# A gated delta net's second pair of head groups gets tiles of its own, and the block solutions move to GpSimd

## The chip, the cores and the metric

The kernel is a decoder of two blocks on one core of a Trainium2 chip. The metric is the device time of one execution in microseconds; the profile shows one execution, its span from the first to the last instruction. TensorE (PE) does the matmuls, VectorE (DVE), ScalarE (ACT) and GpSimd (POOL) work on tiles, SyncE (SP) issues most DMAs; GpSimd issues some. Each engine works through a list of its own in order, and waits on semaphores for the others.

## The reference, cut to what matters

The first block takes 256 tokens of width 1024 and has two mixers side by side. The change is within the first of them, a gated delta rule over 8 heads in chunks of 64:

```
proj = rmsnorm(x) @ w_in          # q, k, v, z, two gates, and the second mixer's inputs
k, q = l2norm(silu(conv(.)));  v = silu(conv(.))
decay = exp(G_i - G_j) below the diagonal;  a_mat = beta * (k k^T) * decay, strictly lower
sol   = (I + a_mat)^-1 @ [v * beta, k * beta * exp(G)]        # triangular_solve, per head and chunk
for each chunk:  v_new = value - k_cum @ s
                 o = (q * exp(G)) @ s + (q k^T * decay) @ v_new
                 s = s * chunk_decay + (k * exp(g_last - G))^T @ v_new
y_a = (rmsnorm(o) * silu(z)) @ w_proj_gdn
y_b = (forgetting attention) @ w_proj_fox
h = x + (sigmoid(gate_a) * y_a + sigmoid(gate_b) * y_b) @ w_out
x = h + relu(h_normed @ w_up)^2 @ w_down
```

A second block (two swiglu layers and another attention mixer) follows and is not touched.

## The kernel before, in words

Activations lie transposed, features on partitions and the 256 tokens on the free axis. Each weight matrix comes in by DMA on SP's queue as `raw`; ACT rounds it to a high part `wh` (L220), DVE subtracts to get the low part `wl` (L221, 128x1024 at a time), and PE does three matmuls of 128x128 by 128x256 for each pair of tiles: high by high, high by low, low by high (L258 to L260 and L349 to L351). A matmul of this kind is called a projection matmul below; one weight unit of 1024 columns is 24 of them.

The first block's code is a set of lines (Python generators) which a planner interleaves: the main line yields the PE time that it puts out, and side lines (the head groups, the solutions) advance between, after the delays that they yield. So the order on each engine is fixed when the program is built. `PLAN` lists what the main line projects: q, k and v of a head group ("heads"), two heads' z, or a sixteenth of the two gates. After it come the second mixer's output projection, then that of the delta rule in two parts: the first (L1135, L1138) takes groups 0 and 1, the second (L1147, L1148) groups 2 and 3.

The eight heads are four groups of two, and two groups are a pair. A group (`gdn_group`) has four instances, a head and 128 tokens each, and goes through these steps: decay rows by a DMA on GpSimd's queue (L619, L621) and exp (L750); products k k^T and q k^T on PE (L761); the matrix `bm` and the masked `at` (L775, L778); `bm` is written out as an image and comes back as 16 diagonal blocks of 32x32 on each partition (L685, L689). With both groups of a pair in, `solve` inverts all blocks: 31 steps of one multiplication and one subtraction (L703, L707), each on up to 80 elements of a partition, in order. The result is stored (L710) and loaded by each group as `xp` (L814). ACT and DVE spread it into `tt`, then come two steps that join blocks to 64x64 (PE L839, L846), the passes through both chunks (`apply`, L860 to L870, and L879 to L886), the output (L899), its norm with an inverse root on GpSimd (L910 and the helper's L146 to L154), and transposes back (L919), which z's values multiply (L921). `nkv` (L784, L785) scales v's transposes on ACT; it comes from an inverse root on GpSimd too, and lies in the small tile `cl`.

Before the change each pair uses one set of tiles for all of this, tagged by the parity of the group: the second pair's groups begin only when the first pair's groups are done (`chain`).

Of the kernel before, what the change touches and what calls it, by code (L numbers as in the profile page):

```python
# [15 lines left out]
P = 128  # L16
T = 256
# [26 lines left out]
for _name, _w in (  # L44
# [10 lines left out]
    [("heads", 0), ("heads", 1), ("z", 0), ("z", 1), ("gate", 0), ("gate", 1), ("gate", 2), ("heads", 2), ("gate", 3)]  # L55
    + [("heads", 3), ("z", 2), ("z", 3)] + [("gate", i) for i in range(4, 8)]
# [611 lines left out]
class Pair:  # L668
# [46 lines left out]
def gdn_group(g, grp, have, zg, pair):  # L715

# [8 lines left out]
    def buf(name):  # L725
        return g.gx.tile([P, 4, P], F32, tag=f"{name}{par}", name=nm(g, name))
# [10 lines left out]
    def small(shape, name):  # L737
        return g.gs.tile(shape, F32, tag=f"{name}{par}", name=nm(g, name))
# [13 lines left out]
    bm = x1  # L752
# [4 lines left out]
    for h in range(2):  # L757
# [4 lines left out]
        for c in range(2):  # L762
            i = 2 * h + c
            nc.vector.tensor_tensor_reduce(
                out=xp[:, i], in0=pq[:, c, 0], in1=g.ident, scale=1.0, scalar=0.0, op0=ALU.mult, op1=ALU.add,
# [13 lines left out]
        yield 0.9, 0.0  # L779
# [6 lines left out]
    yield 0.0, 2.0  # L786
# [830 lines left out]
```

## Time and profile before

| what | us |
|---|---|
| median of 3 runs | 1060.54 (1059.9 to 1066.08) |
| the profiled execution | 1059.77 |
| its span | 1058.0 |
| PE busy | 1006.4 (95%) |
| DVE busy | 695.6 (66%) |
| ACT busy | 558.9 (53%) |
| POOL busy | 204.9 (19%) |

Busy time is a share of the whole span. PE is the engine that the span is made of; which stretch of it holds a wait is told by the windows and the timeline further down.

### The profile page before, as it was taken

How to read it: one execution, taken by the hardware profiler on the slowest of the kernel's cores; microseconds unless marked ns; L12 is line 12 of the kernel's file. 1: busy time of each engine (PE TensorE's matmuls, PEld its weight loads, DVE VectorE, ACT ScalarE, POOL GpSimd, SP SyncE). 2: the span in 40 equal slices, each digit the busy share in tenths (PEclk: the TensorE clock that was granted, in tenths of full speed). 3: DMA queues.
4: the chain of work that ended last, by engine and by line, in shares of the span. 5: the costliest groups of instructions: out<-in, count | busy, mean ns of one | idle time of the engine just before them, and what ended most of it. 6: DMA issues, size and time to landing. Idle time of an engine off the chain costs nothing.

```text
span 1058.0 us, 20140 instructions
## 1 busy us (share of the span) xinstructions
PE 1006.4 (95%) x8126; PEld 976.3 (92%) x8126; DVE 695.6 (66%) x1194; ACT 558.9 (53%) x1000; POOL 204.9 (19%) x379
## 2 busy tenths in 40 slices
PE   8999999999907799999999999999999999999997
PEld 7888999999907799999999999999989899999997
DVE  6676887975773587665555665676775677666553
ACT  6766765645512356654444544435566755444443
POOL 1367250002430320000000111140104511121000
PEclk9999999999957899999999999999999999999999
DMA  8645356554430145555545545457653445554451
GB/s 288 243 176 200 123 187 190 203 169 144 141 97 6 55 185 199 200 181 180 198 174 186 199 171 189 163 192 231 223 189 135 148 157 200 200 199 162 165 179 53
DMA packets 47373, 181.93 MB, mean 172 GB/s; under 512 B 20128, under 2 KB 22576, under 8 KB 29488
## 3 DMA queue, kind: packets, MB, share of 16 engines
q1 hardware_dynamic: 45888, 175.38, 47.9%
q0 software_dynamic: 960, 4.74, 1.3%
q8 instruction: 63, 1.03, 0.4%
q10 hardware_dynamic: 432, 0.53, 0.1%
q14 instruction: 30, 0.25, 0.1%
HBM read 178.25 MB, written 2.38 MB: 171 GB/s over the span
## 4 chain that ended last, share of the span: by engine, by line
PE 65%; DVE 4%; POOL 2%; DMA 1%; ACT 1%; issue 1%; SPq 0%; DVEq 0%; ACTq 0%; POOLq 0%
PE g L259 19%; PE g L258 19%; PE g L260 19%; DVE wl L221 1%; PE g L349 1%; PE g L350 1%; PE g L351 1%; DVE sol L707 1%; DVE stmp L703 1%; PE g L310 1%; PE g L308 1%; PE g L309 1%; PE w L1226 1%; POOL rsq L153 0%; PE w L949 0%
## 5 line engine op out<-in xcount | busy, mean ns | idle before, releaser
L221 DVE TENSOR_TENSOR wl<-raw,wh 128x1024 fp32r<-128x1024 f32 (+2 forms) x347 | 418.6, 1210 | 207.8 <-ACT wh L220 200.8
L220 ACT CAST wh<-raw 128x1024 fp32r<-128x1024 f32 (+2 forms) x347 | 343.7, 995 | 339.0 <-PE g L259 296.4
L260 PE MATMUL g<-Bh,wl 128*128 128x256 f32 x816 | 227.6, 280 | 0.0
L259 PE MATMUL g<-Bl,wh 128*128 128x256 f32 x816 | 227.5, 279 | 0.0
L258 PE MATMUL g<-Bh,wh 128*128 128x256 f32 x816 | 227.0, 279 | 0.0
L260 PE MATMUL g<-Ah,wl 128*128 128x256 f32 x776 | 218.0, 281 | 0.0
L259 PE MATMUL g<-Al,wh 128*128 128x256 f32 x776 | 217.9, 281 | 0.0
L258 PE MATMUL g<-Ah,wh 128*128 128x256 f32 x776 | 217.4, 281 | 0.3 <-DVE fnat L981 0.3
L260 PE MATMUL g<-ah,wl 128*128 128x256 f32 x608 | 170.1, 280 | 1.2 <-DVE wl L221 1.2
L258 PE MATMUL g<-ah,wh 128*128 128x256 f32 x608 | 170.3, 280 | 0.0
L259 PE MATMUL g<-al,wh 128*128 128x256 f32 x608 | 170.2, 280 | 0.0
L258 PEld LDWEIGHTS g<-Bh,wh 128*128 128x128 f32 x816 | 154.4, 190 | 0.1
L259 PEld LDWEIGHTS g<-Bl,wh 128*128 128x128 f32 x816 | 153.2, 188 | 0.2
L260 PEld LDWEIGHTS g<-Bh,wl 128*128 128x128 f32 x816 | 153.2, 188 | 0.1
L260 PEld LDWEIGHTS g<-Ah,wl 128*128 128x128 f32 x776 | 147.1, 190 | 0.1
L258 PEld LDWEIGHTS g<-Ah,wh 128*128 128x128 f32 x776 | 145.7, 188 | 0.8 <-DVE fnat L981 0.7
L259 PEld LDWEIGHTS g<-Al,wh 128*128 128x128 f32 x776 | 145.9, 188 | 0.3 <-DVE Al L411 0.2
L260 PEld LDWEIGHTS g<-ah,wl 128*128 128x128 f32 x608 | 115.5, 190 | 1.4 <-DVE wl L221 1.4
L258 PEld LDWEIGHTS g<-ah,wh 128*128 128x128 f32 x608 | 114.3, 188 | 0.0
L259 PEld LDWEIGHTS g<-al,wh 128*128 128x128 f32 x608 | 114.3, 188 | 0.0
L1196 POOL TENSOR_TENSOR s<-s,row 128x512 f32<-128x512 f32 x22 | 37.7, 1715 | 207.7 <-ACT s L1195 207.7
L427 POOL TENSOR_TENSOR acc<-acc,sq 128x512 f32<-128x512 f32 x10 | 14.1, 1413 | 244.5 <-ACT sq L422 244.5
(321 smaller groups left out, 1387.3 us busy)
## 6 DMA issues: line engine op xcount, KB each, us to landing
raw<-in_w_in_dram SPq DMA_DIRECT2D x44, 1024.0 KB, 4.8
raw<-in_ffn_gu_dram SPq DMA_DIRECT2D x44, 1024.0 KB, 4.7
raw<-in_ffn_dn_dram SPq DMA_DIRECT2D x32, 704.0 KB, 4.0
raw<-in_w_up_dram SPq DMA_DIRECT2D x16, 1024.0 KB, 4.8
raw<-in_w_down_dram SPq DMA_DIRECT2D x16, 1024.0 KB, 4.8
raw<-in_w_out_dram SPq DMA_DIRECT2D x8, 1024.0 KB, 4.8
raw<-in_w_proj_fox_dram SPq DMA_DIRECT2D x4, 1024.0 KB, 4.9
raw<-in_w_proj_gdn_dram SPq DMA_DIRECT2D x4, 1024.0 KB, 4.8
```

Of the source, the lines that this page charges most:

```text
L220: nc.scalar.copy(hi[:, r], raw[:, r])
L221: nc.vector.tensor_tensor(out=lo[:, r], in0=raw[:, r], in1=hi.bitcast(F32)[:, r], op=ALU.subtract)
L258: nc.tensor.matmul(out, lhsT=w_h, rhs=xh[:, k, :], start=(k == 0), stop=False)
L259: nc.tensor.matmul(out, lhsT=w_h, rhs=xl[:, k, :], start=False, stop=False)
L260: nc.tensor.matmul(out, lhsT=w_l, rhs=xh[:, k, :], start=False, stop=(k == nk - 1))
L308: nc.tensor.matmul(ps[b][t], lhsT=a_h, rhs=w_h, start=(k == 0), stop=False)
L309: nc.tensor.matmul(ps[b][t], lhsT=a_l, rhs=w_h, start=False, stop=False)
L310: nc.tensor.matmul(ps[b][t], lhsT=a_h, rhs=w_l, start=False, stop=(k == KT - 1))
L349: nc.tensor.matmul(ps[:, j], lhsT=hi[:, c], rhs=src[0][:, k], start=(i == 0), stop=False)
L350: nc.tensor.matmul(ps[:, j], lhsT=hi[:, c], rhs=src[1][:, k], start=False, stop=False)
L427: e.tensor_tensor(out=acc, in0=acc, in1=sq, op=ALU.add)
L1196: nc.gpsimd.tensor_tensor(out=s, in0=s, in1=u.row2, op=ALU.mult)
```

## The change

The second pair has tiles of its own for `at` and `bm`; `uu`, `tt`, `xp` and `vnew` stay shared, and its groups take them when the first pair's group of the same parity has passed its last use. Up to that point (decay rows, products, image, solution, v's transposes) nothing waits for the first pair but the tiles of the solution, `blk` and `sol`, which the pairs use one after the other. The transposes of q and k and the squares move behind the wait, `k`'s scaled copy lies in `vnew`, the outputs in `bm`, and the product with q is done after the second `apply`. `solve` runs on GpSimd, which also issues the solution's store and its loads. `PLAN` puts the second pair's projections early and z late. The gates lie in four tiles of which the last takes the place of `blk`. Finished groups are merged as the projections go on.

```diff
 PLAN = (
-    [("heads", 0), ("heads", 1), ("z", 0), ("z", 1), ("gate", 0), ("gate", 1), ("gate", 2), ("heads", 2), ("gate", 3)]
-    + [("heads", 3), ("z", 2), ("z", 3)] + [("gate", i) for i in range(4, 8)]
+    [("heads", 0), ("heads", 1), ("gate", 0), ("heads", 2), ("gate", 1), ("heads", 3)]
+    + [("gate", i) for i in range(2, 6)] + [("z", i) for i in range(4)] + [("gate", 6), ("gate", 7)]
 )
...
-    def __init__(self, g):
-        self.g, self.ready, self.done = g, 0, False
-        self.blk = g.gx.tile([P, 32, 32], F32, tag="blk", name=nm(g, "blk"))
-        self.sol = g.gx.tile([P, 32, 8], F32, tag="sol", name=nm(g, "sol"))
-        self.out = g.dr.tile([32, P, 8], F32, tag="solved", name=nm(g, "solved"))
+    def __init__(self, g, before=None):
+        self.g, self.before, self.ready, self.solved, self.done = g, before, 0, False, False
+        self.blk = None
+        self.passed = set()
...
         nc.sync.dma_start(out=image, in_=bm)
         yield 0.0, 3.0
+        while self.before and not self.before.solved:
+            yield 0.0, 0.5
+        if self.blk is None:
+            self.blk = g.gx.tile([P, 32, 32], F32, tag="blk", name=nm(g, "blk"))
...
         self.ready += 1
         if self.ready == 2:
-            g.lines.spawn(self.solve(), 10.0)
+            self.side = g.lines.spawn(self.solve(), 5.0)
 
     def solve(self):
         g, nc = self.g, self.g.nc
-        v = nc.vector
-        sol, blk = self.sol, self.blk
+        gp = nc.gpsimd
+        blk = self.blk
+        sol = g.gx.tile([P, 32, 8], F32, tag="sol", name=nm(g, "sol"))
+        out = self.out = g.dr.tile([32, P, 8], F32, tag="solved", name=nm(g, "solved"))
         tmp = g.gx.tile([P, 80], F32, tag="stmp", name=nm(g, "stmp"))
-        nc.gpsimd.tensor_copy(sol, g.con["eye"].rearrange("p (i c) -> p i c", c=8))
+        gp.tensor_copy(sol, g.con["eye"].rearrange("p (i c) -> p i c", c=8))
         for jj in range(31):
             n, m, w = 31 - jj, jj + 1, jj // 4 + 1
             t = tmp[:, : n * w].rearrange("p (i k) -> p i k", k=w)
-            v.tensor_tensor(
+            gp.tensor_tensor(
                 out=t, in0=blk[:, jj, m:].unsqueeze(2).to_broadcast([P, n, w]),
                 in1=sol[:, jj, 0:w].unsqueeze(1).to_broadcast([P, n, w]), op=ALU.mult,
             )
-            v.tensor_tensor(out=sol[:, m:, 0:w], in0=sol[:, m:, 0:w], in1=t, op=ALU.subtract)
+            gp.tensor_tensor(out=sol[:, m:, 0:w], in0=sol[:, m:, 0:w], in1=t, op=ALU.subtract)
             if jj % 4 == 3:
-                yield 0.0, 1.5
-        nc.sync.dma_start(out=self.out.rearrange("a (n i) c -> (a n) (i c)", n=4), in_=sol.rearrange("p i c -> p (i c)"))
-        yield 0.0, 5.0
+                yield 0.0, 3.0
+        gp.dma_start(out=out.rearrange("a (n i) c -> (a n) (i c)", n=4), in_=sol.rearrange("p i c -> p (i c)"))
+        self.solved = True
+        yield 0.0, 6.0
         self.done = True
...
 def gdn_group(g, grp, have, zg, pair):
...
-    def buf(name):
-        return g.gx.tile([P, 4, P], F32, tag=f"{name}{par}", name=nm(g, name))
+    def buf(name, bufs=1):
+        return g.gx.tile([P, 4, P], F32, tag=f"{name}{par}", name=nm(g, name), bufs=bufs)
...
-    x0, x1, at, uu, tt, xp = (buf(n) for n in ("x0", "x1", "at", "uu", "tt", "xp"))
-
-    kdn = g.gx.tile([P, 2, P], F32, tag=f"kd{par}", name=nm(g, "kd"))
-    dec = x0
+    at = dec = buf("at", 2)
     rows_everywhere(g, dec.rearrange("p (h c) n -> p h (c n)", h=2), h0, 1, g.con["mgdn"], slice(0, 2))
...
-    bm = x1
+    bm = buf("bm", 2)
...
     gp.tensor_scalar_mul(nkv, sk, 0.5)
     gp.tensor_tensor(out=nkv, in0=nkv, in1=r, op=ALU.mult)
     yield 0.0, 2.0
-    pk, pq = bank(), bank()
-    for i, (h, c) in enumerate(inst):
-        nc.tensor.transpose(pq[:, i], kq[:, 1, h, c * P : (c + 1) * P], g.ident)
-    for h in range(2):
-        nc.tensor.transpose(pk[:, h], kq[:, 0, h, 0:P], g.ident)
-    for i in range(4):
-        nc.scalar.activation(out=uu[:, i], in_=pq[:, i], func=AF.Square, accum_out=ss[:, 4 + i : 5 + i])
-    for h in range(2):
-        scale_rows(g, kdn[:, h], pk[:, h], ed[:, h : h + 1])
-
-    gp.tensor_scalar(out=base, in0=ss[:, 4:8], scalar1=P * EPS, scalar2=4 * P * EPS * EPS, op0=ALU.mult, op1=ALU.add)
-    yield 0.66, 4.0
...
     for i in range(4):
         scale_rows(g, vn[:, i], pv[:, i], nkv[:, i : i + 1])
     yield 0.45, 0.0
+    while pair.before and grp - 2 not in pair.before.passed:
+        yield 0.0, 0.3
+    uu, tt, xp, vnew = (buf(n) for n in ("uu", "tt", "xp", "vnew"))
+    kdn = vnew[:, 1:4:2]
+    pk, pq = bank(), bank()
+    for i, (h, c) in enumerate(inst):
+        nc.tensor.transpose(pq[:, i], kq[:, 1, h, c * P : (c + 1) * P], g.ident)
+    for h in range(2):
+        nc.tensor.transpose(pk[:, h], kq[:, 0, h, 0:P], g.ident)
+    for i in range(4):
+        nc.scalar.activation(out=uu[:, i], in_=pq[:, i], func=AF.Square, accum_out=ss[:, 4 + i : 5 + i])
+    for h in range(2):
+        scale_rows(g, kdn[:, h], pk[:, h], ed[:, h : h + 1])
+
+    gp.tensor_scalar(out=base, in0=ss[:, 4:8], scalar1=P * EPS, scalar2=4 * P * EPS * EPS, op0=ALU.mult, op1=ALU.add)
+    yield 0.66, 0.0
     while not pair.done:
         yield 0.0, 0.5
 
     packed = xp[:, 0]
-    nc.sync.dma_start(
+    nc.gpsimd.dma_start(
         out=packed.rearrange("p (a c) -> p a c", c=8), in_=pair.out[16 * par : 16 * par + 16].rearrange("a p c -> p a c")
...
-    vnew, o = x0, tt
+    o = bm
...
     for h in range(2):
         nc.tensor.matmul(ps[:, h], lhsT=kq[:, 0, h, P:T], rhs=st[:, h], start=True, stop=True)
     for h in range(2):
-        nc.tensor.matmul(ps[:, 2 + h], lhsT=kq[:, 1, h, P:T], rhs=st[:, h], start=True, stop=True)
-    for h in range(2):
+    yield 0.45, HOP
+    yield from apply(1)
+
+    ps = bank()
     for h in range(2):
-        scale_rows(g, o[:, 2 * h + 1], ps[:, 2 + h], eg[:, 2 * h + 1 : 2 * h + 2])
-    yield 0.9, HOP
-    yield from apply(1)
+        nc.tensor.matmul(ps[:, h], lhsT=kq[:, 1, h, P:T], rhs=st[:, h], start=True, stop=True)
+    for h in range(2):
+        scale_rows(g, o[:, 2 * h + 1], ps[:, h], eg[:, 2 * h + 1 : 2 * h + 2])
...
     for i in range(4):
-        nc.scalar.activation(out=xp[:, i], in_=o[:, i], func=AF.Square, scale=P ** -0.5, accum_out=so[:, i : i + 1])
-    yield 0.9, 3.0
+        nc.scalar.activation(out=at[:, i], in_=o[:, i], func=AF.Square, scale=P ** -0.5, accum_out=so[:, i : i + 1])
+    pair.passed.add(grp)
+    yield 1.35, 3.0
...
-        gates = [gp.tile([P, KT, T], F32, tag=f"gate{w}", name=f"gate{w}") for w in range(2)]
-        pair = Pair(g)
-        groups, zs = [ln.spawn(gdn_group(g, i, haves[i], zg, pair)) for i in range(2)], set()
+        gates = [gp.tile([P, 4, T], F32, tag=f"gate{w}", name=f"gate{w}") for w in range(3)]
+        pairs = [Pair(g)]
+        pairs.append(Pair(g, pairs[0]))
+        groups, zs = [ln.spawn(gdn_group(g, i, haves[i], zg, pairs[0])) for i in range(2)], set()
-        pairs = []
-
-        def chain(i, have, before):
-            while not before[i - 2].done:
-                yield 0.0, 0.3
-            if not pairs:
-                pairs.append(Pair(g))
-            yield from gdn_group(g, i, have, zg, pairs[0])
+        def gate(w, m):
+            return gates[2 * w + m // 4][:, m % 4 : m % 4 + 2]
...
+                if i == 6:
+                    ln.finish(pairs[1].side)
+                    gates.append(g.gx.tile([P, 4, T], F32, tag="blk", name="gate3"))
...
-                    groups.append(ln.spawn(chain(i, have, groups[:])))
+                    groups.append(ln.spawn(gdn_group(g, i, have, zg, pairs[1])))
...
+        merged = []
+
+        def merge(upto, wait):
+            while len(merged) < upto and (wait or groups[len(merged)].done):
+                i = len(merged)
+                ln.finish(groups[i])
+                m = 2 * i
+                split_act(g, oh[:, m : m + 2], ol[:, m : m + 2], zg[:, m : m + 2])
+                merged.append(i)
...
-            if m < 4:
-                heads(m // 2)
+            merge(2, False)
+        merge(2, True)
...
+            merge(4, False)
 
         yield from project_part(g, (oh, ol), (0, 1, 2, 3), 2, first)
-        heads(2)
-        heads(3)
+        merge(4, True)
```

On GpSimd, at the end of the first solution. After the change (`sol`, `stmp`, `blk` are the solution's tiles, `xp` those of groups 0 and 1, `cl_2089` the small tile of group 2 with `nkv`):

```order
L154 TENSOR_TENSOR cl_2089<-cl_2089,rsq_2385 128x4
L709 TENSOR_TENSOR stmp_1992<-blk_1827,sol_1990 128x24
L790 TENSOR_TENSOR cl_2089<-cl_2089 128x4
L713 TENSOR_TENSOR sol_1990<-sol_1990,stmp_1992 128x24
L709 TENSOR_TENSOR stmp_1992<-blk_1827,sol_1990 128x16
L713 TENSOR_TENSOR sol_1990<-sol_1990,stmp_1992 128x16
L709 TENSOR_TENSOR stmp_1992<-blk_1827,sol_1990 128x8
L713 TENSOR_TENSOR sol_1990<-sol_1990,stmp_1992 128x8
L716 DMA solved_1991<-sol_1990 128x256
L824 DMA xp_1911<-solved_1991 128x16x8
L824 DMA xp_1964<-solved_1991 128x16x8
L705 COPY sol_2699<-con 128x256
```

Before, GpSimd has at that place the clearing of `sol` and `xp` alone, and then the second pair's decay rows:

```order
L699 COPY sol_3024<-con 128x256
L833 MEMSET xp_1609 128x8x32
L833 MEMSET xp_1618 128x8x32
L850 MEMSET xp_1609 64x256
L850 MEMSET xp_1618 64x256
L619 DMA x_435_3026<-rowsd 128x2x256
L619 DMA x_443_3047<-rowsd 128x2x256
```

The 62 steps and three DMAs stand on GpSimd now, with the second pair's norm chain between the steps.

On ACT, in the same stretch, after the change (`vt_1658` is v of group 2, `kq_2175` k and q of group 3, `tt_1910` and `tt_1963` the spread solutions of groups 0 and 1):

```order
L220 CAST wh_2462<-raw_2408 128x1024
L170 ACTIVATE cacc_2333<-g_2258,par 128x256
L170 ACTIVATE vt_1658<-w_2426,cl_2089 128x128 x4
L220 CAST wh_2525<-raw_2523 128x1024
L639 ACTIVATE kq_2175<-cacc_2251 128x256
L639 ACTIVATE kq_2175<-cacc_2333 128x256
L220 CAST wh_2557<-raw_2523 128x1024
L170 ACTIVATE cacc_2340<-g_2258,par 128x256
L170 ACTIVATE cacc_2447<-g_2347,par 128x256
L220 CAST wh_2587<-raw_2585 128x1024
L1118 ACTIVATE gate_1589<-g_2461 128x512
L170 ACTIVATE tt_1910<-xp_1911,con 128x4x32 x2
```

Before, the head projections' activations there stood among weight splits alone, and the spread solutions followed them:

```order
L220 CAST wh_2941<-raw_2866 128x1024
L639 ACTIVATE kq_2427<-cacc_2620 128x256
L220 CAST wh_2971<-raw_2969 128x1024
L664 ACTIVATE zg<-g_2813 128x512
L639 ACTIVATE vt_2428<-cacc_2712 128x256
L170 ACTIVATE cacc_2719<-g_2627,par 128x256
L170 ACTIVATE tt_1608<-xp_1609,con 128x4x32 x2
L170 ACTIVATE tt_1617<-xp_1618,con 128x4x32 x2
L220 CAST wh_3001<-raw_2969 128x1024
L220 CAST wh_3064<-raw_3062 128x1024
```

Now the scaling of v by `cl_2089` stands ahead of the weight splits and of `kq_2175`.

On ACT, later, after the change (`xp_3116` and `tt_3115` are the second pair's solution, group 2; `bm_1680`, `vnew_1965` and `at_1602` belong to groups 0 and 1):

```order
L170 ACTIVATE vnew_1912<-w_3038,cl_1682 128x128 x2
L170 ACTIVATE bm_1680<-w_3080,eg 128x128 x2
L220 CAST wh_3321<-raw_3269 128x1024
L914 COPY bm_1680<-w_3085 128x2x128
L919 ACTIVATE at_1602,so_3092<-bm_1680 128x128 x2
L814 ACTIVATE uu_3114,ss_2088<-w_3119 128x128 x3
L919 ACTIVATE at_1602,so_3092<-bm_1680 128x128 x2
L814 ACTIVATE uu_3114,ss_2088<-w_3119 128x128
L170 ACTIVATE tt_3115<-xp_3116,con 128x4x32 x2
L220 CAST wh_3369<-raw_3367 128x1024
L664 ACTIVATE zg<-g_3240 128x512
L170 ACTIVATE vnew_1965<-w_3043,cl_1701 128x128 x2
```

Before, the spreading of the second pair's solution came behind all of the first pair's work:

```order
L170 ACTIVATE vt_2102<-w_3368,cl_3121 128x128 x4
L220 CAST wh_4013<-raw_3779 128x1024
L170 ACTIVATE vt_2428<-w_3383,cl_3139 128x128 x4
L220 CAST wh_4048<-raw_4046 128x1024
L170 ACTIVATE tt_3030<-xp_3031,con 128x4x32 x2
L170 ACTIVATE tt_3051<-xp_3052,con 128x4x32 x2
L170 ACTIVATE x_435_3026<-w_3866,cl_3121 128x128 x2
L170 ACTIVATE x_443_3047<-w_3871,cl_3139 128x128 x2
```

The copy of the second solution stands now ahead of updates and outputs of group 1.

## Rows read from the trace of the kernel before

**Rows 1.** The page, part 2: clock granted to PE, tenths, 40 slices.

```profile
PEclk9999999999957899999999999999999999999999
```

**Rows 2.** Windows around the idle stretch: engines' busy us, PEclk, DMA share, GB/s.

```profile
core 0: us, PE busy (x) PEld busy (x) DVE busy (x) ACT busy (x) POOL busy (x), PEclk, DMA share, GB/s
290.00:317.00 27.00, 2.76 (x25) 2.56 (x23) 18.82 (x67) 4.05 (x10) 8.93 (x21) 0.60 0.40 98
317.00:344.00 27.00, 20.67 (x120) 19.60 (x120) 10.19 (x26) 8.02 (x31) 1.63 (x6) 0.70 0.09 6
```

**Rows 3.** PE's timeline at the ends of that stretch: start, us, instruction, [idle before].

```profile
292.48 0.28 PE L351 MATMUL g<-Ah,wl 128*128 128x256 f32 x1
...
321.34 3.67 PE L839 MATMUL w<-tt,x 128*128 128x64 f32 x16 [28.58 <-ACT tt L170]
...
348.89 2.64 PE L919 MATMUL w<-con,tt 128*128 128x128 f32 x8 [6.88 <-ACT tt L170]
351.73 0.58 PE L349 MATMUL g<-Ah,wh 128*128 128x256 f32 x1 [0.20 <-ACT Ah L175]
```

**Rows 4.** Windows of a few us, columns as in rows 2.

```profile
330.00:335.00 5.00, 5.00 (x28) 4.63 (x27) 1.96 (x5) 1.14 (x4) 0.00 (x0) 0.71 0.00 0
...
356.00:358.00 2.00, 2.00 (x16) 2.00 (x16) 0.00 (x0) 0.00 (x0) 0.00 (x0) 0.79 0.00 0
...
268.00:270.00 2.00, 1.11 (x10) 0.92 (x9) 0.36 (x1) 0.00 (x0) 2.00 (x14) 1.00 0.56 131
270.00:272.00 2.00, 1.11 (x6) 0.95 (x7) 0.00 (x0) 1.56 (x6) 0.78 (x5) 1.00 0.93 393
```

**Rows 5.** PE's timeline, first pair's steps and projection matmuls at full clock.

```profile
143.68 3.62 PE L761 MATMUL w<-kq 128*128 128x256 f32 x16
...
204.70 0.28 PE L258 MATMUL g<-Ah,wh 128*128 128x256 f32 x1
...
205.04 0.28 PE L258 MATMUL g<-Ah,wh 128*128 128x256 f32 x1
...
220.00 2.23 PE L839 MATMUL w<-tt,x 128*128 128x64 f32 x16
...
241.87 0.61 PE L884 MATMUL w<-xp,kq 128*128 128x128 f32 x4
242.31 0.61 PE L886 MATMUL w<-xp,kq 128*128 128x128 f32 x4
```

**Rows 6.** Timelines of GpSimd and DVE, and a group of GpSimd's by line.

```profile
83.83 0.20 POOL L152 TENSOR_TENSOR rsq<-rsq 128x8 f32<-128x8 f32 x1
...
85.29 0.23 POOL L153 TENSOR_SCALAR rsq<-rsq 128x8 f32<-128x8 f32 x1
...
152.17 1.23 POOL L152 TENSOR_TENSOR rsq<-rsq 128x4 f32<-128x4 f32 x1
...
152.12 1.20 DVE L221 TENSOR_TENSOR wl<-raw,wh 128x1024 fp32r<-128x1024 f32 x1
...
L621 POOL TENSOR_TENSOR x<-x,con 128x512 f32<-128x512 f32 x4 | 5.1, 1282 | 3.4 <-DMA x<-rowsd 3.4
```

**Rows 7.** DVE's timeline: first and last step of the solutions (first pair's, second pair's).

```profile
167.02 0.19 DVE L703 TENSOR_TENSOR stmp<-blk,sol 128x31 f32<-128x31 f32 x1 [2.81 <-DMA blk<-img]
...
210.12 0.16 DVE L707 TENSOR_TENSOR sol<-sol,stmp 128x8 f32<-128x8 f32 x1
...
301.73 0.19 DVE L703 TENSOR_TENSOR stmp<-blk,sol 128x28 f32<-128x28 f32 x1
...
315.42 0.17 DVE L707 TENSOR_TENSOR sol<-sol,stmp 128x8 f32<-128x8 f32 x1
```

**Rows 8.** DMAs: issue time on GpSimd by line, and us from issue to landing.

```profile
L619 POOL DMA_DIRECT2D x<-rowsd x4 | 3.0, 762 | 36.5 <-PE w L899 30.1 <-ACT Bh L175 6.4
...
x<-rowsd POOLq DMA_DIRECT2D x4, 256.0 KB, 4.2
...
xp<-solved SPq DMA_DIRECT2D x4, 64.0 KB, 3.4
```

More of the change, by code (lines that the diff above doesn't have):

```diff
@@ L764, in gdn_group @@
             nc.vector.tensor_tensor_reduce(
-                out=xp[:, i], in0=pq[:, c, 0], in1=g.ident, scale=1.0, scalar=0.0, op0=ALU.mult, op1=ALU.add,
+                out=bm[:, i], in0=pq[:, c, 0], in1=g.ident, scale=1.0, scalar=0.0, op0=ALU.mult, op1=ALU.add,
                 accum_out=sk[:, i : i + 1],
@@ L778, in gdn_group @@
             nc.vector.tensor_tensor(out=at[:, i], in0=pq[:, c, 1], in1=dec[:, i], op=ALU.mult)
-        yield 0.9, 0.0
+        yield 0.9, 3.0 * h
     yield from pair.load(par, bm)
@@ L786, in gdn_group @@
     yield 0.0, 2.0
+    while "v" not in have:
+        yield 0.0, 0.3
+    vt = have["v"]
+    pv = bank()
+    for i, (h, c) in enumerate(inst):
+        nc.tensor.transpose(pv[:, i], vt[:, h, c * P : (c + 1) * P], g.ident)
+    vn = vt.rearrange("p h (c n) -> p (h c) n", c=2)
+    for i in range(4):
+        scale_rows(g, vn[:, i], pv[:, i], nkv[:, i : i + 1])
+    yield 0.45, 0.0
+    while pair.before and grp - 2 not in pair.before.passed:
+        yield 0.0, 0.3
+    uu, tt, xp, vnew = (buf(n) for n in ("uu", "tt", "xp", "vnew"))
+    kdn = vnew[:, 1:4:2]
     pk, pq = bank(), bank()
@@ L797, in gdn_group @@
     gp.tensor_scalar(out=base, in0=ss[:, 4:8], scalar1=P * EPS, scalar2=4 * P * EPS * EPS, op0=ALU.mult, op1=ALU.add)
-    yield 0.66, 4.0
-    while "v" not in have:
-        yield 0.0, 0.3
-    vt = have["v"]
-    pv = bank()
-    for i, (h, c) in enumerate(inst):
-        nc.tensor.transpose(pv[:, i], vt[:, h, c * P : (c + 1) * P], g.ident)
-    vn = vt.rearrange("p h (c n) -> p (h c) n", c=2)
-    for i in range(4):
-        scale_rows(g, vn[:, i], pv[:, i], nkv[:, i : i + 1])
-    yield 0.45, 0.0
+    yield 0.66, 0.0
     while not pair.done:
@@ L914, in gdn_group @@
     yield 0.0, 8.0
-    ps = raw_bank().rearrange("p (h t) -> p h t", h=2)
     while grp not in g.zs:
         yield 0.0, 0.3
+    ps = raw_bank().rearrange("p (h t) -> p h t", h=2)
     for i, (h, c) in enumerate(inst):
@@ L1113, in start @@
                 def start(i=i, have=have):
-                    groups.append(ln.spawn(chain(i, have, groups[:])))
+                    groups.append(ln.spawn(gdn_group(g, i, have, zg, pairs[1])))
                 yield from gdn_project(g, u, i, have, start)
         oh, ol = xpair(g, "A")
-        def heads(i):
-            ln.finish(groups[i])
-            m = 2 * i
-            split_act(g, oh[:, m : m + 2], ol[:, m : m + 2], zg[:, m : m + 2])
+        merged = []
[6 more added lines that the diff above has]
+                merged.append(i)
         for m in range(0, KT, 2):
             ps = yield from gemm_pair(g, ob, KT)
-            gt = gates[1][:, m : m + 2]
+            gt = gate(1, m)
             nc.vector.scalar_tensor_tensor(out=gt, in0=gt, scalar=1.0, in1=ps, op0=ALU.add, op1=ALU.mult)
-            if m < 4:
-                heads(m // 2)
+            merge(2, False)
+        merge(2, True)
         def first(m, ps):
-            gt = gates[1][:, m : m + 2]
+            gt = gate(1, m)
             t = g.sq.tile([P, 2, T], F32, tag="sq", name=nm(g, "zt"))
-            nc.vector.scalar_tensor_tensor(
-                out=t, in0=gates[0][:, m : m + 2], scalar=1.0, in1=ps, op0=ALU.add, op1=ALU.mult
-            )
+            nc.vector.scalar_tensor_tensor(out=t, in0=gate(0, m), scalar=1.0, in1=ps, op0=ALU.add, op1=ALU.mult)
             nc.gpsimd.tensor_tensor(out=gt, in0=gt, in1=t, op=ALU.add)
+            merge(4, False)
         yield from project_part(g, (oh, ol), (0, 1, 2, 3), 2, first)
-        heads(2)
-        heads(3)
+        merge(4, True)
         mh, ml = xpair(g, "B")
         def second(m, ps):
-            gt = gates[0][:, m : m + 2]
+            gt = gate(0, m)
             nc.vector.scalar_tensor_tensor(out=gt, in0=gt, scalar=1.0, in1=ps, op0=ALU.add, op1=ALU.mult)
-            (nc.gpsimd if m < 4 else nc.vector).tensor_tensor(out=gt, in0=gt, in1=gates[1][:, m : m + 2], op=ALU.add)
+            (nc.gpsimd if m < 4 else nc.vector).tensor_tensor(out=gt, in0=gt, in1=gate(1, m), op=ALU.add)
             split_act(g, mh[:, m : m + 2], ml[:, m : m + 2], gt)
@@ L1158, in first_block @@
         nf = F1 // P
-        ah = operand(act, nf, 0, "ah", "ah")
-        al = operand(act, nf, 0, "al", "al")
+        ah = operand(act, nf, 4, "ah", "ah")
+        al = operand(act, nf, 60, "al", "al")
         late = Late(g, ln.spawn(hn.scales(), 1.5), 1)
```

6 lines of the change are left out of this document (2 added, 4 removed).

## The prediction

> **What bounds the kernel now.** I read the busy lines in 40 slices first. PE is busy in nine tenths of nearly every slice; what is lost lies in slices 13 to 15, where its clock falls too [rows 1]. The windows over that place come next: between 290 and 317 us PE works 2.76 us of 27, DVE 18.82 [rows 2]. PE's timeline then shows where the time goes. The first part of the output projection starts its last matmul at 292.48; PE then idles 28.58 us for the second pair's solution, does that pair's steps, idles 6.88 us more for its norm, and starts the second part at 351.73 [rows 3]. So the second pair, from its solution to its end, lies alone on the path: 351.73 - 292.76 = 59.0 us. Around it a little more is lost. The granted clock is 0.79 over 356 to 358, so PE stays at the lower level (0.50, 1.2 GHz) until about 356.8; 5.1 us at half speed lose 2.6. At 268 to 272 PE works 2 x 1.11 us of 4.00, which loses 1.8 [rows 4].
>
> **What the change can take away at most.** The second pair's PE work remains and takes PE's time wherever it stands. For both groups, counted as the trace does (two for each of these fp32 matmuls in the code), it is 32 matmuls of 128x64, 88 of 128x128 and 8 transposes. The first pair did the same at full clock: 2.23 us for the first 16, as much for the next; four of 128x128 took from 241.87 to 242.31, so 0.11 each, 9.7 for 88 [rows 5]; the transposes about 1.2 (2.64 at half clock [rows 3]). Together about 15 us. If all of it lies among other matmuls and nothing new waits, the span falls by 59.0 + 2.6 + 1.8 - 15 = 48.4, to 1058.0 - 48.4 = 1009.6.
>
> **What is removed.** The second pair no longer waits for the first: its decay rows, products and images have tiles of their own (one DMA and four exponentials per group stand earlier, on GpSimd's queue and ACT), and its second half of steps waits only until a first-pair group has passed. The q and k transposes, the squares and k's scaling (6 PE and 6 ACT instructions a group) move behind that wait; the q product moves behind the second half's update. All of these stand among projections that fill PE, and I cost them at nothing: their cover is gem work of 0.1135 us a matmul (204.70 to 205.04 for three [rows 5]). Of SP's queue the solution's store and the loads of it go to GpSimd's; there the second pair's blk loads now wait for the first solution's end, with four weight loads behind them. The first of those weights is used 147 matmuls, 16.7 us of PE's work, behind the place where I let PE wait for the same solution (S1 below), so SP goes on before PE does and no weight comes late: nothing. A longer solution stops PE as well, so this cover stays; without it each weight would come its 4 to 5 us late.
>
> **What the solution costs on GpSimd.** The trace of before has no such operation on GpSimd, so I bound it. The solution is 62 operations, each waiting on the result of the one ahead, with 3,120 elements per partition in sum. GpSimd's own dependent small operations begin 0.29 us apart (83.83 to 85.29, five steps), and a 128x512 two-input operation takes 1.28 us, so 2.1 ns for each element beyond a handful [rows 6]. 62 x 0.29 + 2,600 x 2.1 ns = 18.0 + 5.5 = 23.5 us alone. On DVE alone it was 58 operations from 301.73 to 315.42, 0.24 each, 14.9 for 62 [rows 7]: the lower end. For the upper end I take the fixed part twice: 41 us.
>
> Beside DVE's work it is longer. A GpSimd operation that overlaps DVE's weight split took 1.23 instead of 0.20 us: it ended with the split that ran 152.12 to 153.32 [rows 6]. Such a split comes with every 24 matmuls (2.72 us), so it holds GpSimd 1.03 of 2.72; the convolution's closing operations, 0.33 each, one to a split in the head projections, hold it more: together half the time. The first solution was under that load on DVE also: 167.02 to 210.12, 43 us [rows 7].
>
> The Trainium skill has a rule against this move. Its page "GPSIMD Engine Reference" (4.1 Engine selection) wants elementwise work on VectorE, GpSimd being about half as fast. The rows above give 0.38 against 0.24 us, less than twice; with twice, 29.8 us alone, the sum would be that of the second rival. Its page "SBUF — State Buffer" (Who interferes with whom) says that the two engines' shared port is held for a whole instruction, with which the row at 152.17 agrees.
>
> **First new wait (S1).** The first solution has its blocks when before had them, at about 167 [rows 7]. Under load for 19 us it does 9.7 us of its 23.7 (the second pair's short norm chain is mixed in); then ACT stops. ACT's scaling of vt by cl_2089 needs GpSimd's last operation on cl_2089, which stands near the end of the solution in GpSimd's order (the ACT order above), and behind ACT's scaling stand its weight splits and the activations that finish the fourth group's k (kq_2175). With the splits stopped DVE falls silent and GpSimd runs alone: 14 us more, to about 200; ACT's five instructions, 2.4 us, bring k to PE at 202.4. PE, from the place of the first k products (143.68 [rows 5]) onward, has 342 projection matmuls and two times 16 pair products with two sets of transposes (3.62 us for 16, about 8.4 in all) until the first that needs this k: 143.2 + 38.8 + 8.4 = 190.4. Idle 12.0. After the long idle of before PE had half clock from 321.34 to about 332.9 (granted 0.71 over 330 to 335), after the short one from 348.89 to 356.8 [rows 3, 4]: 5.8 and 4.0 us lost; I take 4.5. S1 = 16.5. From below zero (a solution of 15 us ends before 190.4 if ACT is not held); from above 34 with 41 us.
>
> **Second new wait (S2).** The second solution's blocks come behind the fourth group's products, 398 projection matmuls after the first k products (143.2 + 45.2 + 10 of pair work + S1 = 215); with decay scaling, image and block loads, the fourth group's norm chain and two clears ahead of it on GpSimd, it starts at about 232. There the splits do run: 23.7 us alone become 30, to 262. Then its store, the load of it, ACT's copy, first products. The store and load took 3.4 us each on SP's queue; GpSimd's queue lands at 4.2 for the decay rows, and issuing one took 0.76 [rows 8], so 2 x 4.7. The load is 2,048 pieces of 32 B; if GpSimd pays by the piece as for the decay rows' 256 (3 ns), it is 6 us to issue. I take 0.76 with 1.5 beside it, since the row is a measured issue, and keep 6 for the range. In ACT's order the copy from this load (tt_3115) stands ahead of an update of the first pair (vnew_1965), which PE wants 717 projection matmuls behind the first k products: 143.2 + 81.4 + 24.7 of pair work + S1 = 265.8. ACT delivers at 275: idle 9 + 1.5 and 4.5 of clock, S2 = 15. Bounds: zero, if nothing is held, to 32 with 41 us and the piecewise issue.
>
> **Third (S3).** At the end of the first part the second pair's norm chain on GpSimd stands between the gate additions, as before, where it cost 6.88 [rows 3]; I keep 6 for it, between 0 and 12.
>
> **Sum.** 1009.6 + 16.5 + 15 + 6 = 1047.1 span; the profiled execution has 1.77 us around its span (1059.77 with 1058.0), so 1048.9 against 1059.77. The median of the runs shown is 0.77 above that profiled one: 1049.6. I forecast 1049, its own range 1040 to 1058. A measurement of this kernel tells about 1% from no change: the bounds are 1050 and 1071, and the forecast lies at the first.
>
> **Rivals.**
> First, GpSimd isn't held as long: it slips between DVE's operations and the solution takes 24 to 26 us in place. For it: only one of the small operations in the rows is stretched. Against: DVE's order is fixed and its splits are always there. S1 falls to about 3, S2 to 5, S3 to 2, with no clock loss: 1009.6 + 10 + 2.6 = 1022.
> Second, the operation costs twice DVE's 0.24 (0.48, 29.8 us alone). Each solution ends 6 us later, and each wait is longer by as much: 1049 + 12 = 1061, no change. For it: two-input operands with broadcast strides, which no GpSimd row has. Against: 0.29 is measured with dependence in it.
> Third, slower: the fixed part is twice 0.29, so 41 us alone. Each wait grows by 17: 1049 + 34 = 1083. It decides at both places where ACT stands behind the solution (cl_2089, tt_3115). The point from which the kernel is slower at all is 6 us per solution, 0.48 an operation; over 1% slower from 11 each, 0.56. The piecewise load issue alone, 5.3 us more at each of two loads of either pair, of which three stand ahead of a wait, gives 1049 + 16 = 1065, which is within 1%.
> That the change doesn't do what it says is excluded by the order: the second pair's solution and its steps do stand ahead of the first part's end.
>
> **How the numbers follow.** Forecast 0.50, half of it below 1050 and a little more, 0.28 to 0.22; first rival 0.22; second, the load's price with it, 0.16; third 0.12. Faster by over 1%: 0.28 + 0.22 = 0.50; within: 0.22 + 0.16 = 0.38; slower 0.12. The range leaves out the lower half of the first rival and most of the third: 1022 to 1072. The likeliest is 1049.
>
> **What would show it.** In the changed kernel's trace: the solution's operations on GpSimd start 0.37 us apart on average where DVE is silent, and near 0.6 beside splits; PE idles about 12 us near 190, released by ACT behind cl_2089; about 10 near 266, released by ACT's vnew behind the solution's load; about 6 ahead of the second part; no idle over 3 us elsewhere, and none released by a weight. Wrong if operations start over 0.48 us apart, if PE idles in one of the places for the DMA of the solution, or if it waits for weights behind SP's blk load.

## The result, and the profile after

The changed kernel takes 1045.95 us (median of 4, 1044.6 to 1051.67) against 1061.03 for the kernel before on the same chip: ratio 0.986, 95% interval 0.981 to 0.991. That is 15 us less; the forecast was 1049. The profiled execution took 1044.6 us with a span of 1042.8, 15.2 less than before.

PE's timeline after answers to [rows 3]. These are its waits of over 1 us up to the second part of the projection (its steps from L349 stand for both parts), with two shorter ones that the sum further down uses:

```profile
199.29 2.07 PE L766 MATMUL w<-kq 128*128 128x256 f32 x4 [8.44 <-DVE kq L640]
...
210.38 1.13 PE L766 MATMUL w<-kq 128*128 128x256 f32 x4 [1.31 <-DVE kq L640]
...
269.17 2.08 PE L911 MATMUL w<-vnew,at 128*128 128x128 f32 x8 [6.49 <-ACT vnew L170]
...
328.90 0.62 PE L932 MATMUL w<-con,bm 128*128 128x128 f32 x2 [2.53 <-ACT bm L170]
330.07 0.77 PE L932 MATMUL w<-con,bm 128*128 128x128 f32 x2 [0.55 <-ACT bm L170]
...
332.34 1.22 PE L349 MATMUL g<-Ah,wh 128*128 128x256 f32 x4 [1.49 <-ACT Ah L175]
339.75 0.72 PE L349 MATMUL g<-Ah,wh 128*128 128x256 f32 x4 [1.50 <-ACT Ah L175]
...
349.34 0.39 PE L285 MATMUL g<-Bl,wh 128*128 128x256 f32 x1 [0.65 <-DVE Bl L176]
```

The 28.58 and 6.88 us are gone; in their place stand a wait at the fourth group's products, one at the first pair's outputs, and short ones where the second pair ends. The second part begins at 332.34 where it began at 351.73. ACT's timeline tells why PE waits at 199.29 (first two rows below: it stood 10.75 us for `cl`, with splits and `kq` behind; PE's row names DVE, which does the last operation on `kq` after ACT's) and at 269.17 (last two: it stood for the solution's load, with `vnew` behind):

```profile
195.24 1.14 ACT L170 ACTIVATE vt<-w,cl 128x128 f32<-128x128 f32 x4 [10.75 <-POOL cl L790]
...
197.18 0.75 ACT L639 ACTIVATE kq<-cacc 128x256 f32<-128x256 f32 x2
...
266.27 0.92 ACT L170 ACTIVATE tt<-xp,con 128x128 f32<-128x128 f32 x2 [8.88 <-DMA xp<-solved]
...
268.51 0.60 ACT L170 ACTIVATE vnew<-w,cl 128x128 f32<-128x128 f32 x2
```

On GpSimd's timeline are the two solutions, from 164.88 to 196.5 and from 230.48 to 259.6. The rows answer to [rows 6, 7]:

```profile
164.88 0.24 POOL L709 TENSOR_TENSOR stmp<-blk,sol 128x31 f32<-128x31 f32 x1 [5.22 <-DMA blk<-img]
...
168.06 1.26 POOL L709 TENSOR_TENSOR stmp<-blk,sol 128x28 f32<-128x28 f32 x1
...
196.34 0.20 POOL L713 TENSOR_TENSOR sol<-sol,stmp 128x8 f32<-128x8 f32 x1
196.84 0.65 POOL L716 DMA_DIRECT2D solved<-sol  x1 [0.30 <-POOL sol L713]
200.82 2.32 POOL L824 DMA_DIRECT2D xp<-solved  x2 [3.32 <-DMA solved<-sol]
...
230.48 0.24 POOL L709 TENSOR_TENSOR stmp<-blk,sol 128x31 f32<-128x31 f32 x1 [7.73 <-DMA blk<-img]
...
251.17 0.30 POOL L709 TENSOR_TENSOR stmp<-blk,sol 128x66 f32<-128x66 f32 x1
251.55 0.32 POOL L713 TENSOR_TENSOR sol<-sol,stmp 128x66 f32<-128x66 f32 x1
251.95 0.29 POOL L709 TENSOR_TENSOR stmp<-blk,sol 128x60 f32<-128x60 f32 x1
...
259.38 0.20 POOL L713 TENSOR_TENSOR sol<-sol,stmp 128x8 f32<-128x8 f32 x1
```

Undisturbed, operations on 60 to 66 elements start 0.38 to 0.40 us apart (251.17 to 251.95); over the 53 undisturbed steps of the second solution the mean is 0.36. The operation at 168.06 took 1.26: DVE's split ran from 168.02 to 169.24.

```profile
168.02 1.22 DVE L221 TENSOR_TENSOR wl<-raw,wh 128x1024 fp32r<-128x1024 f32 x1
```

The Trainium skill's page "SBUF — State Buffer" (Who interferes with whom) has the port that both engines share locked for a whole instruction; this row agrees, and eight operations of the first solution and seven of the second took over 1 us, 9.8 and 8.5 us together. Its page "GPSIMD Engine Reference" (4.1 Engine selection) calls GpSimd about twice as slow for two-input work. For the same 62 multiplications the median here is 0.29 us on GpSimd against 0.21 on DVE (`e2` below has the solution there), a factor of 1.4. The view of line L709 of the changed kernel (duration ns min/median/max, first and last start):

```profile
L709 POOL TENSOR_TENSOR stmp<-blk,sol x62: 202/290/1372, 164.9 to 259.1; 128x60 f32<-128x60 f32 x6, 128x28 f32<-128x28 f32 x4, 128x54 f32<-128x54 f32 x4, 128x48 f32<-128x48 f32 x4
```

and with the solution on DVE:

```profile
L709 DVE TENSOR_TENSOR stmp<-blk,sol x62: 167/210/239, 164.7 to 268.5; 128x60 f32<-128x60 f32 x6, 128x28 f32<-128x28 f32 x4, 128x54 f32<-128x54 f32 x4, 128x48 f32<-128x48 f32 x4
```

Windows at the three stalls show the clock's return, and for the third its fall (0.85 over 329 to 331, so at 330.4; columns as in [rows 2]):

```profile
203.00:205.00 2.00, 2.00 (x15) 2.00 (x14) 0.88 (x1) 0.00 (x0) 1.13 (x2) 0.72 0.93 348
...
271.00:273.00 2.00, 2.00 (x14) 2.00 (x13) 1.40 (x3) 1.48 (x5) 1.09 (x5) 0.66 0.00 0
...
329.00:331.00 2.00, 1.29 (x4) 0.50 (x4) 0.12 (x1) 2.00 (x8) 1.03 (x4) 0.85 0.12 45
...
336.00:338.00 2.00, 2.00 (x15) 2.00 (x13) 0.00 (x0) 1.28 (x4) 0.37 (x2) 0.69 0.00 0
```

PE worked at the lower level (0.50, 1.2 GHz) from 199.29 to about 204.1, from 269.17 to 272.4 and from 330.4 to 337.2, of which the wait ahead of 332.34 is 1.49. Half of PE's time at work in these stretches is lost: 2.4, 1.6 and 2.7 us.

### The profile page after: what moved, and what is told of

It reads as the page before. It is cut to its first block, busy times and chain, and to the rows that moved or that the text cites. A ratio compares the mean times of both kernels' runs of the same rounds, so it can differ in the third digit from the quotient of the medians.

```text
span 1042.8 us, 20129 instructions
## 1 busy us (share of the span) xinstructions
PE 1005.7 (96%) x8126; PEld 976.3 (94%) x8126; DVE 673.5 (65%) x1070; ACT 557.0 (53%) x1000; POOL 262.6 (25%) x509
```

## The experiments

Theory A: the tiles and the order bring the gain, and what is still lost comes from instructions that ACT (or another queue) has in order behind GpSimd's solution. Theory B: k or the weights are late because GpSimd and DVE hold each other. Theory C: moving the solution to GpSimd is what gains. Ratios are to the kernel before on the same chip.

**The parts of the change.** Three kernels take it apart. `e2_solve_dve` is the changed kernel with

```diff
-        gp = nc.gpsimd          # solve
+        gp = nc.vector
-        gp.dma_start(out=out...)           # store; the loads of xp likewise
+        nc.sync.dma_start(out=out...)
```

> The changed kernel, with the solutions back on DVE and their store and loads back on SP's queue; own tiles and order stay. Theory A (the tiles and the order bring the gain, GpSimd's solution only costs): the first solution takes 40 us or so beside DVE's splits, but ACT no longer waits for it, since the norm chain on GpSimd is free; the second ends near 255 to 262; 1036 to 1048, no slower than the changed kernel by over 3 us. Theory C (the move to GpSimd is the gain): the first solution holds DVE's splits and the second the first pair's steps, 1054 or more.

Measured: 1037.34 us, ratio 0.976 (0.974 to 0.979), faster than the whole change. On PE's timeline no product of the second pair (L766) waits over 0.2 us; the first solution is waited for 2.06 and 1.36, the end 5.26:

```profile
230.29 1.10 PE L849 MATMUL w<-tt,bm 128*128 128x64 f32 x8 [2.06 <-ACT tt L170]
...
324.19 1.35 PE L932 MATMUL w<-con,bm 128*128 128x128 f32 x4 [5.26 <-ACT bm L170]
```

The solutions are not done sooner on DVE: the first ends at 222.4 there and at 196.5 on GpSimd, the second at 268.9 and 259.6. But the order of instructions is set anew when a kernel is built, and it changed with the engine. From the first k products to the first step that needs the solution (L849), PE starts 470 matmuls in the changed kernel and 705 in `e2`. So `e2` undoes the move together with the order that came with it, and no run tells the two apart.

`e3_before_pool` makes the opposite edit in the kernel before:

```diff
-        v = nc.vector           # solve
+        v = nc.gpsimd
-        nc.sync.dma_start(out=self.out...)     # store; the loads of xp likewise
+        nc.gpsimd.dma_start(out=self.out...)
```

> The kernel before, with the solutions on GpSimd and their store and loads on its queue, and nothing else of the change. Theory A: the second solution lies alone on the path, took 19.7 us on DVE with its first splits and takes 23.5 to 28 on GpSimd, the loads 1 to 2 us more: 1064 to 1071, slower by 4 to 10 us. Theory C: 1052 or less.

Measured: 1067.55, ratio 1.005 (1.004 to 1.007): 5.5 us slower, in the range, but not where I had put it. Here too the order moved: PE starts 446 matmuls up to the first step that needs the solution, 658 before. It waits 11.09 us there for the first solution (at 207.02; before, no step of this kind waited over 0.12), and 23.65 for the second (at 328.56; 28.58 before). The second part began at 358.45 instead of 351.73. `e13_old_plan` keeps all of the change but `PLAN`:

```diff
-    [("heads", 0), ("heads", 1), ("gate", 0), ("heads", 2), ("gate", 1), ("heads", 3)]
+    [("heads", 0), ("heads", 1), ("z", 0), ("z", 1), ("gate", 0), ("gate", 1), ("gate", 2), ("heads", 2), ("gate", 3)]
...
```

> The changed kernel with the order of projections of before (z early, the fourth group 192 matmuls later). If the own tiles alone make the gain, it stays near 1046. If the order is needed too, the second solution ends near 285 to 290 and the second pair's chain of 50 us or so runs past the end of the first part (305): 15 to 30 us of idle time there, 1052 to 1062.

Measured: one execution of 1049.48, below the range I gave: by it 11.5 of the 15 us remain with the old order. PE waits 7.94 us for the first solution (at 208.85), 5.46 for the first pair's norm, whose chain on GpSimd stands between the steps of the second solution (275.70), and 6.27 for the second pair's end (335.43). So theory C falls on both sides: all of the change but the move gives 24.7 us (`e2`), and the move, with its order, takes 9.6 of them back (0.986 against 0.976; the intervals do not meet). What the new `PLAN` adds to the tiles is not shown: its 3.5 us, by one execution, lie within the spread of the changed kernel's own four.

**What stands behind the solution.** In `e8_key_chain_dve` the second pair's norm chain of k is on DVE:

```diff
-    rsqrt_cols(g, r, sk, f"rsq{par}")
-    gp.tensor_scalar_mul(nkv, sk, 0.5)
+    key = nc.vector if pair.before else gp
+    rsqrt_cols_on(g, key, r, sk, f"rsq{par}")
+    key.tensor_scalar_mul(nkv, sk, 0.5)      # and the product with r
```

> The changed kernel, with the second pair's norm chain of k (13 small operations a group) on DVE in place of GpSimd; so v's scaling on ACT waits for no GpSimd operation, and all else stays. Theory A: the 8.44 us at the fourth group's products fall under 2, the wait at the first pair's outputs stays or grows (6 to 11 us, since PE is there earlier): 1034 to 1040. Theory B: 5 us or more stay at the products, 1043 to 1049.

In `e1_v_behind` the wait for the first pair stands ahead of v's transposes instead of behind their scaling:

```diff
+    while pair.before and grp - 2 not in pair.before.passed:
+        yield 0.0, 0.3
     while "v" not in have:
...
-    while pair.before and grp - 2 not in pair.before.passed:
-        yield 0.0, 0.3
```

> The changed kernel, with the second pair's transposes and scaling of v moved behind the wait for the first pair. Then ACT meets neither cl_2089 nor tt of the second solution ahead of work that PE waits for. Theory A (ACT's order behind GpSimd's solution makes both waits): the idle time at the fourth group's products (8.44 + 1.31 us) and at the first pair's outputs (6.49) both fall under 2 us each, with their half clock (2.4 and 1.6); of these 20 us some 4 come back in the second pair's own chain, which gets longer by the scaling: 1030 us, 1026 to 1036. Theory B (k or the weights are late because the solution's operations and DVE's hold each other): 5 us or more of idle time stay at the fourth group's products, 1041 to 1048.

Measured: 1048.21 (0.987, 0.985 to 0.988) and 1049.33 (0.988, 0.987 to 0.990), no gain. By number this looks like theory B: 15.77 and 14.93 us stay at the products. The rows say otherwise. In `e8` PE's timeline has this wait:

```profile
215.26 2.08 PE L766 MATMUL w<-kq 128*128 128x256 f32 x4 [15.77 <-DVE kq L640]
```

and ACT's, in the same run, this one ahead of it:

```profile
209.85 0.51 ACT L170 ACTIVATE tt<-xp,con 128x128 f32<-128x128 f32 x1 [16.07 <-DMA xp<-solved]
```

ACT no longer stops at `cl`. It goes on to the next instruction that needs the solution, the spreading `tt<-xp`, which stands in its order ahead of the second k activation, and stops there for longer. In `e1` ACT is done with k at 193.6, ahead of the spreading; there DVE, which spreads the other half, stands in the same way ahead of its last operation on `kq` (211.70):

```profile
210.83 0.56 DVE L833 TENSOR_SCALAR tt<-xp,con 128x128 f32<-128x128 f32 x2 [16.58 <-DMA xp<-solved]
```

My expectation took one waiting instruction, on one engine, for the whole line of them.

`e9_order_first` changes order alone. `issue_after` queues instructions behind another on its engine and adds no wait, and the lines hold these steps back until that place has been reached, so PE's transposes of v come later too:

```diff
+    if tile_idx == 23:              # conv_silu: fourth group's last v
+        g.marks = (a, d)            # its ACT and its DVE instruction
+    with behind(g, g.marks ...):    # v's scaling of the second pair; spreading of the first pair's xp
+        ...                         # behind(): g.tc.issue_after(a), g.tc.issue_after(d)
```

> The changed kernel, with an edge of order alone (no wait): on ACT and DVE the second pair's v scaling and the spreading of the first pair's solution are queued behind the fourth group's last convolution. The two runs that took only the wait for cl_2089 away had it come back at the spreading of the first solution. Theory A (whatever stands in ACT's or DVE's order behind GpSimd's solution stops the fourth group): with both behind, idle time at the fourth group's products is under 2 us and no other wait of over 4 us takes its place before 230 us; 1036, between 1030 and 1041. Theory B (the products are late for GpSimd's hold on DVE, or for weights): 5 us or more stay there, 1043 to 1050.

`e10_order_both` queues the second pair's spreading behind the first pair's outputs as well:

```diff
+    pair.marks = (amark, dmark)     # last square of the outputs on ACT, last output sum on DVE
+    with behind(g, pair.before.marks if pair.before else g.marks):    # the spreading
```

> As the kernel with the first solution queued behind the fourth group, and the spreading of the second pair's solution is queued on ACT and DVE behind the first pair's outputs too. Theory A: the 6.49 us at the first pair's outputs go as well; what is left is the second pair's chain at the end, which starts some us later: 1033, between 1028 and 1038. Theory B: no faster than the changed kernel by over 3 us.

Measured: 1040.19 (0.981, 0.979 to 0.982) and 1034.82 (0.976, 0.974 to 0.977). Both lie in the range of theory A, and at the two places that it names it holds: nothing is left at the products, in `e10` nothing at the first pair's outputs either. But its condition for `e9`, no other wait of over 4 us before 230 us, failed. A wait of 7.12 us came up in `e9` and of 8.41 in `e10`, both at the first pair's own next step:

```profile
214.34 0.69 PE L864 MATMUL w<-tt,bm 128*128 128x64 f32 x2 [7.12 <-ACT tt L170]
```

```profile
215.05 0.69 PE L864 MATMUL w<-tt,bm 128*128 128x64 f32 x2 [8.41 <-ACT tt L170]
```

ACT had met the same event at a weight ahead of that step, for 11.52 us in `e9`, and in `e10`:

```profile
209.96 1.04 ACT L220 CAST wh<-raw 128x1024 fp32r<-128x1024 f32 x1 [13.39 <-DMA raw<-in_w_in_dram]
```

That weight's load stands on SP behind the second pair's `blk`, which waits for the first solution's end. In `e10` ACT then waited 0.92 us more for the second load of the solution. `e14_blk_off_sp` is `e10` with this edit, `e17_blk_only` is the changed kernel with it:

```diff
-            nc.sync.dma_start(out=self.blk[p0 : p0 + 16], in_=diag)
+            (nc.gpsimd if self.before else nc.sync).dma_start(out=self.blk[p0 : p0 + 16], in_=diag)
```

> The kernel with both order edges, and the second pair's blk loads (8 DMAs, which wait for the end of the first solution) issued by GpSimd in place of SP, so that weight loads no longer stand behind them. In the run before it ACT's splits waited 13.4 us for a weight there and PE 8.41. Theory A (three things stand in line behind the first solution's end: ACT's scaling, ACT's spreading, SP's weight loads): with the third moved PE's idle time near 215 falls under 3 us; 1034.8 less 8 with its half clock: 1027, between 1023 and 1031. Rival (GpSimd's 8 issues push the solution's store and the second solution back by as much): 1032 to 1037.

> The changed kernel as it is, with only the second pair's blk loads issued by GpSimd. As the prediction has it, weights that wait behind blk on SP cost nothing there, since PE is stopped by ACT for the same solution: within 3 us of the changed kernel, 1043 to 1049. If SP's wait costs in the changed kernel itself: 1041 or less.

Measured: `e14` 1036.91 (0.976, 0.971 to 0.980), no gain over `e10`; `e17` 1042.91 (0.982, 0.979 to 0.985), 3 us under the changed kernel and just under the range I gave. Its interval overlaps the changed kernel's, so a gain there is neither shown nor excluded; 8.41 us stay at the products. In `e14` ACT waits for no weight any more, but 12.18 us for the solution itself, whose store now stands on GpSimd behind four blk issues of 2.64 us together; the load behind it is issued at 211.79, in `e10` at 205.38. GpSimd's timeline of `e14`, then ACT's, then PE's:

```profile
202.10 2.64 POOL L695 DMA_DIRECT2D blk<-img  x4
204.73 0.59 POOL L718 DMA_DIRECT2D solved<-sol  x1
211.79 2.33 POOL L836 DMA_DIRECT2D xp<-solved  x2 [6.47 <-DMA solved<-sol]
```

ACT, spreading the first solution:

```profile
215.80 1.92 ACT L170 ACTIVATE tt<-xp,con 128x128 f32<-128x128 f32 x4 [12.18 <-DMA xp<-solved]
```

PE, at the first pair's own next step:

```profile
216.76 0.69 PE L864 MATMUL w<-tt,bm 128*128 128x64 f32 x2 [9.93 <-ACT tt L170]
```

So the rival of that run came true. Last in line is what the solution is for: PE's step L864, the same that waited in `e9` and `e10`. In `e2` this step (L849 there) stands later in PE's order and waits 2.06; that order was not tried with the solution on GpSimd.

**Prices and the end.** `e11_loads_on_sp` is the changed kernel with store and loads on SP's queue again:

```diff
-        gp.dma_start(out=out...)               # store; the loads of xp likewise
+        nc.sync.dma_start(out=out...)
```

> The changed kernel, with the solution's store and loads back on SP's queue; the solution stays on GpSimd. If the loads issued by GpSimd are what costs, each of two loads lands 2 to 3 us earlier and the waits behind them shrink: 1040 to 1044. If GpSimd's queue costs little, and SP's weight loads stand behind a store that waits for the solution: 1045 to 1050.

Measured: 1044.57 (0.985, 0.983 to 0.987), between the two ranges and no difference that can be told; the loads landed after 3.8 us (median) instead of 5.4, and the waits are 7.78 at the products and 7.76 at 262.09. `e15_last_norm_dve` is `e14` with the second pair's last norm chain on DVE, `e16_solve_dve_ordered` is `e15` with the solutions on DVE (`gp = nc.vector` in `solve`, as in `e2`, store and loads still on GpSimd):

```diff
+    late = nc.vector if pair.before else gp
-    rsqrt_cols(g, r2, so, f"rsq{par}")
+    rsqrt_cols_on(g, late, r2, so, f"rsq{par}")      # and the sum ahead of it
```

> As the run beside it, with the second pair's last norm chain (14 small operations a group) on DVE. If the chain on GpSimd between the gate additions is what is late at the end (4.14 us at the transposes back): 3 us less than the run beside it, 1024, 1020 to 1028. If DVE's splits hold it up as long: no faster than that run.

> As the run beside it with the last norm on DVE, with both solutions on DVE again; their store and loads stay on GpSimd's queue. Theory A: once nothing that PE needs stands in order behind the solution, its engine matters little: within 4 us of that run. If GpSimd's slowness itself costs: faster by over 4. If DVE's time is what is short (solution beside splits): slower by over 4.

Measured: 1039.56 (0.979, 0.976 to 0.981) and 1035.99 (0.976, 0.973 to 0.978). The chain on DVE did not help: the wait at the transposes back is 4.21 after 4.13. The chain's 0.16 us operations lie there between splits of 1.21 and gate products, and three of them took 1.09 to 1.26, each ending with an addition of the gates on GpSimd. DVE's row, then GpSimd's:

```profile
318.06 1.26 DVE L154 TENSOR_TENSOR r<-r,rsq 128x4 f32<-128x4 f32 x1
```

```profile
318.03 1.28 POOL L1171 TENSOR_TENSOR gate<-gate,zt 128x512 f32<-128x512 f32 x1 [2.25 <-DVE rsq L153]
```

So either engine held up the other. With both order edges the solution's engine matters by 3.6 us, with intervals that overlap, less than the 9.6 of before, which is what theory A asked for; here too PE's order moved with it (517 matmuls up to the step that needs the solution in `e15`, 808 in `e16`). The fastest kernels, `e10`, `e14`, `e16` and `e2`, lie within 3 us of each other.

## Why the prediction was right

**The bound (48.4).** Stalls and half clock after sum to 30.1 us by the rows: 12.2 (S1: 8.44 + 1.31 + 2.4), 8.1 (S2: 6.49 + 1.6), 9.1 (S3, below) and 0.7 of waits under 1 us. With 1009.6 that gives 1039.7 of the measured 1042.8, so the bound was some 3 us too low. Of these, 1.1 lies at an edit that I had not costed at all: the relu layer's operands `ah` and `al` now begin 4 and 60 elements into their tiles, and that stretch took 91.4 us, from 463.26 to 554.66, where it took 90.3 before (479.31 to 569.64). That the offset is the cause was not tried apart. Some 0.7 lies in the stretch ahead of it, where PE's matmuls start further apart than before (last section); the rest is not placed. One reading of [rows 1] was off by one, with nothing resting on it: the low digits are the 12th to the 14th.

**The solution.** 0.38 us alone was forecast, 0.36 to 0.38 is seen; 33 and 30 us in place were forecast, 31.6 and 29.1 measured. The first solution was held for less than the half of the time that the working had: from 164.88 until ACT stopped 33 operations began, 0.59 us apart, where 9.7 us at 0.38 make 25. The first rival (not held) and the second (0.48 an operation) both fall by these rows, the third with them. The issue of a load took 1.16 us, not the 0.76 that I chose, and not the 6 of the other bound.

**S1** was the right chain, from ACT's scaling behind `cl_2089` to `kq_2175`, 8.44 us where 12.0 stood. The solution began 2 us earlier than I had it and k came 3 earlier. The clock cost 2.4, since it was back after 4.8 us of work; I had taken 4.5 from two stalls of before, of which even the shorter, 6.88 us, was followed by 7.9 us at the lower level. Why that shorter one cost more than the 8.44 us here no row shows.

**S2** was the right chain too, `tt_3115` ahead of `vnew_1965`: 6.49 where 10.5 stood, clock 1.6 where 4.5 stood. Store and load took 6.4 us (259.88 to 266.27) where 9.4 and 1.5 stood.

**S3** was undersized: 9.1 for 6. Its waits are near what I had: 2.53, 0.55 and 1.49 us ahead of the second part, 1.50 and 0.3 in and behind it (0.65, of which 0.32 was there before), 6.4 together. They come in two lots, since the fourth group's end follows the third's by some 8 us, where before both groups came in together. The 2.7 of the clock had no term: my sum took away the half clock behind the wait of before and put none back for this one.

**SP's wait costs nothing** is what the trace of the changed kernel shows, where PE stood for ACT and no split waited for a weight; the 3 us of `e17` are not told from nothing. But "a longer solution stops PE as well, so this cover stays" holds only as long as ACT is stopped: with ACT free it waited 13.4 us for a weight (`e10`). Whether PE lost by that is open, since its own step waited for the same solution and `e14` was no faster.

**The size.** PE stood at the three places that were named, over 3 us nowhere else, and never for a weight. That the number came so near, 1046 for 1049, is in part luck: S1 and S2 were too large by 11 us together, S3 too small by 3, and the bound with its small waits too low by nearly 4.

**The sign** is explained by the parts: the change without the move gains (`e2`; most of it with the old `PLAN` too, by one execution of `e13`), and the move to GpSimd, with the order that it brings, is a smaller loss.

## What to carry to other kernels

When a long serial step moves to another engine, list every queue that has an instruction behind its result (here ACT's scaling, ACT's and DVE's spreading, SP's loads): taking one away moves the wait to the next, for the same event and about the same length, and one edit alone measures as little or no change. An engine that is idle is not free if a busy one holds it up, here 15 operations of the two solutions by some 0.9 us each. Undoing that part of a change by itself told more than all the reasons around it; but count the instructions ahead of the step in question as well, since the order on the other engines may change with it.

## What the runs showed of the hardware that had not been expected

At a granted clock of 1.00 PE's projection matmuls do not always start 0.1135 us apart [rows 5]. Read off PE's timeline, stretches of 0.113 alternate with stretches of 0.118. In the kernel before, six matmuls take 0.68 us near 380 and 0.71 near 450:

```profile
379.76 0.28 PE L258 MATMUL g<-Bh,wh 128*128 128x256 f32 x1
...
380.44 0.28 PE L258 MATMUL g<-Bh,wh 128*128 128x256 f32 x1
```

```profile
449.74 0.28 PE L259 MATMUL g<-Al,wh 128*128 128x256 f32 x1
...
450.45 0.28 PE L259 MATMUL g<-Al,wh 128*128 128x256 f32 x1
```

After the change they take 0.71 near 380, as already from 350 on, and in the relu stretch ten take 1.19, 0.119 each:

```profile
379.78 0.28 PE L259 MATMUL g<-Al,wh 128*128 128x256 f32 x1
...
380.49 0.28 PE L259 MATMUL g<-Al,wh 128*128 128x256 f32 x1
```

```profile
499.72 0.28 PE L258 MATMUL g<-ah,wh 128*128 128x256 f32 x1
...
500.91 0.28 PE L259 MATMUL g<-al,wh 128*128 128x256 f32 x1
```

The step from 0.113 to 0.118 is 4% of PE's time in such a stretch, and no run here shows what sets it.
